# A two-block network on one core: modulation moved into the first mixing, an embedding's projection in fp32 ahead of the FFNs, and the context FFN ended ahead of the second FFN

## The chip, the core and the metric

The kernel runs on one core of a Trainium2 chip. A core has TensorE (matmul, written PE, with its weight load PEld), VectorE (DVE), ScalarE (ACT), GpSimd (POOL) and SyncE (SP, which here issues most of the DMAs). The metric is the device time of one execution in microseconds. Three timed runs of the kernel before gave a median of 2905.65 us (2905.5 to 2906.85).

## The reference

One call takes a latent of 256 tokens of width 1024 through two blocks. `first_block` has two layers:

```python
h = h + mixing(rmsnorm(h))     # layer 0: RWKV recurrence + Hyena; layer 1: neighbourhood attention
h = h + conv_ffn(h, ...)       # (gelu(u[:2816]) * u[2816:]) @ w_down, u = dwconv(rmsnorm(h) @ w_up)
h = h + sigmoid(rmsnorm(h) @ w_gate) * (p_i @ w_proj)      # per-layer embedding, p_i is 256 x 256
```

`second_block` has two layers with a second stream, the context of 256 tokens. Each layer is a half-FFN, a token mixing and another half-FFN, and every norm is modulated:

```python
ml = split(silu(c) @ w_mod[l] + b_mod[l], 9)        # latent; mc is the same with c_ctx, for the context
x   = half_ffn(x,   g_norm[l,0], ml[0], ml[1], ml[2], ...)
ctx = half_ffn(ctx, g_norm[l,0], mc[0], mc[1], mc[2], ...)
```

The modulation needs only `c`, `c_ctx` and `w_mod`, and the context's first half-FFN needs only `ctx` and the modulation. So both can be computed at any time ahead of their use, beside the first block. The same holds for `p_i @ w_proj`.

## The kernel before

**Layout and products.** Activations lie with features on the partitions, as [128, 8, 256] (eight tiles of 128 features by 256 tokens). Nearly every product is made as three matmuls of a reduced-precision fp32 type (`fp32r`). An fp32 weight tile is loaded into a `raw` buffer and split into a high part, a cast on ScalarE (L359), and a low part, a subtraction on VectorE or GpSimd (L360). The activation is split the same way. `gemm` then adds three products: high by high (L368), high by low (L369) and low by high (L370). `gemm_wide` (L406 to L408) does so for four weight tiles at a time, for the start of a stage behind a norm. `plain` (L397) is the other form: the fp32 weight and the fp32 activation go into one matmul as they are, with no split. `plain_tiles` (L372) loads for it and takes its buffers from the pool `self.whole`, 512 columns each.

**Buffers.** From the first FFN on, weights arrive in four `raw` buffers of 128 x 1024 fp32. The split parts lie in pairs `wh`, `wl`: two pairs in `wha`, which live for the whole kernel, and some in `whb`, which a stage opens for itself. PSUM has eight banks; until the first embedding of the second layer is over, four hold the main products (`mm`), two the norms (`aux`) and two the context FFN (`fill`).

**Stages.** `run` (L1437) writes out the first mixing (`mix`), the first FFN (`conv_ffn(0)`), the first embedding (`embed(0)`), the attention (`na`), the second FFN and the second embedding; then come the stages of the second block. A scheduler of the framework orders each engine's instructions by their place in the program and by when their operands and buffers come free in a timeline that it estimates. So work that stands late in the program is drawn forward into gaps. An instruction given to `keep_in_program_order` is not.

**Work drawn forward.** Two kinds of it matter here. The first is the context FFN. `ctx_ffn` (L948) is a generator of eight pieces with its own buffers and PSUM banks. Four pieces (`CUT`) are written last in `mix`; the rest stand behind the second embedding (L1487), so in the program they come after all six first stages, and the scheduler draws them forward. The second is the modulation. `mod_until` (L1004) computes it in steps, 36 a layer. A step loads two tiles of `w_mod` (128 x 1024) and reduces each against `silu(c)` and `silu(c_ctx)`, which lie in `sc` on all partitions. In `mix` the steps 0 to 11 are written ahead of the context FFN, which needs them: each tile comes on GpSimd's DMA queue into a `wha` buffer and takes two reductions on VectorE (L1032). In the FFNs the steps 12 to 19 and 20 to 25 are spread over the groups. There each tile comes on SP's queue into a `wm` buffer. VectorE makes one reduction. The other is a product on GpSimd (L1036), a sum on ScalarE (L1037) and an add on VectorE (L1038). Later stages do the rest of the 72 steps in the same way.

**FFN.** `conv_ffn` (L532) has 22 pairs of up-tiles in three groups. Each pair goes through a convolution over tokens (L527 to L529), gelu, a product and a split (`mh`, `ml`); after a group come its down-products, added to `H` (L568). Ahead of it all stands the norm: `norm1` (L511) takes the root that `rows` makes of the sums of squares (L454), by some small VectorE operations (L424 to L441), spreads it with a matmul against the identity (L480) and scales each tile (L519).

**Embedding.** `embed` (L572) first projects `p_i`: it splits it (`ph`, `pl`), and for each of eight tiles of `ple_p` it loads, splits and multiplies, two chunks deep, then writes half of the product to `pj`. Then comes the norm, the gate's first four tiles in `gemm_wide`, the other four one by one, and the residual add.

Of the kernel before, what the change touches and what calls it, by code (L numbers as in the profile page):

```python
# [10 lines left out]
F32R = mybir.dt.float32r  # L11
I32 = mybir.dt.int32
AF = mybir.ActivationFunctionType
ALU = mybir.AluOpType
# [3 lines left out]
P = 128  # L18
D = 1024
T = 256  # L20
KT = 8
FF = 2816
FT = 22
# [5 lines left out]
DEPTH = 2  # L29
M00 = 32  # L30
CUT = 4
DECAY = math.exp(-0.5)


# [238 lines left out]
class Net:  # L273
# [98 lines left out]
    def plain_tiles(self, name, todo):  # L372


        arr = self.ap[name]
        i = 0
        while i < len(todo):
            t, k0, kn = todo[i]
            n = kn * P
            m = 1  # L380
            while i + m < len(todo) and (m + 1) * n <= 512 and todo[i + m] == (t + m, k0, kn):
                m += 1
            raws = []
            for c in range(0, n, 512):
                w = min(512, n - c)
                raw = self.t(self.whole, [P, 512], "raw")
                src = arr[t : t + m, :, k0 * P + c : k0 * P + c + w].rearrange("t p n -> p t n")
                self.nc.sync.dma_start(raw[:, : m * w].rearrange("p (t n) -> p t n", t=m), src)
                raws.append(raw)
            for j in range(m):  # L390
                yield t + j, lambda k, at=j * n: raws[(at + k * P) // 512][:, (at + k * P) % 512 :][:, :P]
            i += m
# [136 lines left out]
        nc.vector.scalar_tensor_tensor(out[:, 0 : n - 1], src[:, 1:n], w[2], out[:, 0 : n - 1], op0=ALU.mult, op1=ALU.add)  # L529


    def conv_ffn(self, i, mods):  # L532
        nc = self.nc
        with ExitStack() as es:
            pool = self.pool(es, "ffn")
            self.whl_open(es, 0, 3)
            it = self.wtiles(f"f_up{i}", range(2 * FT), KT)
            first = self.first(it, 4)
            xh, xl = self.norm1(pool, f"ffn_norm{i}")
            self.mod_open(pool, True)  # L540
            mod0 = self.mod_at
            outs = [self.acc()[:, :T] for _ in range(4)]
            self.gemm_wide(outs, first, KT, xh, xl)
            for k0, kn in GROUPS:
                mh = self.t(pool, [P, 8, T], "mh", F32R)
                ml = self.t(pool, [P, 8, T], "ml", F32R)
                for j in range(kn):
# [12 lines left out]
                    nc.scalar.activation(u[:, 0], u[:, 0], AF.Gelu_apprx_tanh)  # L560
                    nc.vector.tensor_mul(u[:, 0], u[:, 0], u[:, 1])
                    self.split(u[:, 0], mh[:, j], ml[:, j])
                    if k0 + j > 1:
                        self.mod_until(mod0 + (mods - mod0) * (k0 + j) // (FT - 1))
                for m, wh, wl in self.pieces(f"f_dn{i}", [(m, k0, kn) for m in range(KT)]):
                    ps = self.acc()[:, :T]
                    self.gemm(ps, wh, wl, kn, mh, ml)
# [1 line left out]
                    if k0 == 16:  # L569
                        self.sq_add(m)  # L570

    def embed(self, i):  # L572
        nc = self.nc
        with ExitStack() as es:
            pool = self.pool(es, "ple")
            self.whl_open(es, 0, 3)
            ph = self.t(pool, [P, 2, T], "ph", F32R)
            pl = self.t(pool, [P, 2, T], "pl", F32R)
            pr = self.t(pool, [P, 2, T], "pr")
            nc.sync.dma_start(pr, self.ap[f"p{i}"])  # L580
            self.split(pr, ph, pl)
            pj = self.t(pool, [P, KT, T], "pj")
            m = 0
            for _, wh, wl in self.pieces(f"ple_p{i}", [(t, 0, 2) for t in range(KT)]):
                ps = self.acc()
                self.gemm(ps[:, :T], wh, wl, 2, ph, pl)
                nc.scalar.mul(pj[:, m], ps[:, :T], 0.5)
                m += 1
            it = self.wtiles(f"ple_g{i}", range(KT), KT)
            first = self.first(it, 4)  # L590
            xh, xl = self.norm1(pool, f"ple_norm{i}")
            outs = [self.acc()[:, :T] for _ in range(4)]
            self.gemm_wide(outs, first, KT, xh, xl)
            for m in range(KT):
                if m < 4:
                    ps = outs[m]
                else:
                    ps = self.acc()[:, :T]
                    _, wh, wl = next(it)
                    self.gemm(ps, wh, wl, KT, xh, xl)  # L600
                s = self.t(pool, [P, T], "sg", bufs=2)
                nc.scalar.activation(s, ps, AF.Tanh, scale=0.5)
                nc.vector.scalar_tensor_tensor(s, s, 1.0, pj[:, m], op0=ALU.add, op1=ALU.mult)
                nc.vector.tensor_add(self.H[:, m], self.H[:, m], s)
                self.sq_add(m)

# [232 lines left out]
    def mix(self, ef):  # L839
# [3 lines left out]
        nc = self.nc  # L843
        with ExitStack() as es:
# [4 lines left out]
            with ExitStack() as e2:  # L849
# [82 lines left out]
                self.tag = self.aux = "fill"  # L932
                self.mod_until(12)
                self.rest = self.ctx_ffn(fp)
                for _ in range(CUT):
                    next(self.rest)

    def out0(self, k0, kn, y, last=False):

# [497 lines left out]
    def run(self, es, stages=None):  # L1437
# [30 lines left out]
        self.raw = self.pool(es, "raw", bufs=4)  # L1468
        self.nrm = self.pool(es, "nrm", bufs=6)
        self.rsp = self.pool(es, "rsp", bufs=2)  # L1470
        ep = es.enter_context(ExitStack())
        self.psum_open(ep, mm=4, aux=2, fill=2)
        if "modall" in st:
# [7 lines left out]
                    self.sq_add(k, q)  # L1481
        for s in st:
            if s.startswith("ffn"):
                self.conv_ffn(int(s[3]), 20 if s == "ffn0" else 26)
            elif s.startswith("ple"):
                self.embed(int(s[3]))
                if s == "ple1" and self.own:  # L1487
                    self.tag = self.aux = "fill"
                    for _ in self.rest:
                        pass  # L1490
# [1 line left out]
                    ef.close()  # L1492
                    ep.close()
                    self.psum_open(es, mm=5, aux=3)
            elif s == "na":
                self.na()
            elif s[0] == "h":
# [261 lines left out]
```

## Time and profile before

| | |
|---|---|
| median of three runs | 2905.65 us |
| profiled execution, and its span | 2907.19 us, 2905.4 us |
| granted clock of TensorE | 0.968 |
| busy: PE, DVE, ACT, POOL | 2767.0 us (95%), 1978.3 us (68%), 1216.2 us (42%), 396.7 us (14%) |
| DMA | 143 GB/s in the mean |
| mixing / first FFN / first embedding | to 537 us / 537 to 770 / 770 to 806 |
| attention / second FFN / second embedding | 806 to 1031 / 1031 to 1232 / 1232 to 1262 |
| second block | from 1262 us to the end |

The trace is of one profiled execution. The span goes from the first instruction to the last. An engine's busy time counts the time in which at least one of its instructions ran. The stages' bounds are the times at which TensorE goes over from the one stage's products to the next; work drawn forward from later stages runs inside them.

### The profile page before, as it was taken

To read this page: it belongs to the slowest core of one execution; us is meant where nothing else is said; L and a number is where in the kernel's file an instruction comes from. 1 tells how busy PE (TensorE), PEld (TensorE's weight loads), DVE (VectorE), ACT (ScalarE), POOL (GpSimd) and SP (SyncE) were. 2 spreads that over 40 slices of the span, in tenths; PEclk is the share of its full clock that TensorE was granted. 3 is DMA by queue.
4 is the path that set the end of the run, shared out by engine and by line. 5 is a ranking of instruction groups with operands and counts; after the bars stand their busy time and mean duration, and the time that the engine had idled before them with its cause. 6 is when DMAs were issued, how large, how long until landed. Compare 5 with 4: busy or idle time off the path is not lost.

```text
span 2905.4 us, 49052 instructions
## 1 busy us (share of the span) xinstructions
PE 2767.0 (95%) x19514; PEld 2441.6 (84%) x19514; DVE 1978.3 (68%) x3569; ACT 1216.2 (42%) x2120; POOL 396.7 (14%) x276
## 2 busy tenths in 40 slices
PE   6998999899999989989999999999999999999999
PEld 4676788899899889979988669888898888895999
DVE  5875755789976688867754665777755655567655
ACT  3212223555545555555554454222243222455543
POOL 0100000322542411221211001000010000121100
PEclk8998999999999999989999999999999999999999
DMA  4441223666455356547732103555535444230564
GB/s 164 126 141 58 81 83 117 211 214 221 165 179 159 107 189 203 185 142 241 223 113 68 47 30 119 186 196 179 163 110 164 141 142 134 79 117 25 175 188 139
DMA packets 150807, 415.91 MB, mean 143 GB/s; under 512 B 31585, under 2 KB 51698, under 8 KB 149682
## 3 DMA queue, kind: packets, MB, share of 16 engines
q1 hardware_dynamic: 146258, 393.89, 42.3%
q0 software_dynamic: 4320, 18.88, 1.9%
q8 instruction: 154, 2.52, 0.4%
q14 instruction: 75, 0.61, 0.1%
HBM read 411.66 MB, written 1.05 MB: 142 GB/s over the span
## 4 chain that ended last, share of the span: by engine, by line
PE 73%; DVE 8%; issue 4%; ACT 2%; DMA 1%; POOL 0%; ACTq 0%; DVEq 0%; SPq 0%; POOLq 0%
PE mm L368 18%; PE mm L370 18%; PE mm L369 18%; DVE wl L360 3%; PE fill L370 2%; PE fill L368 2%; PE mm L407 2%; PE mm L1413 2%; PE fill L369 2%; PE mm L408 2%; PE mm L406 2%; PE mm L1381 1%; PE aux L459 1%; ACT wh L359 1%; PE aux L1407 1%
## 5 line engine op out<-in xcount | busy, mean ns | idle before, releaser
L359 ACT CAST wh<-raw 128x1024 fp32r<-128x1024 f32 (+3 forms) x652 | 606.8, 938 | 1016.3 <-PE mm L369 560.8
L360 DVE TENSOR_TENSOR wl<-raw,wh 128x1024 fp32r<-128x1024 f32 (+3 forms) x582 | 712.6, 1228 | 321.3 <-ACT wh L359 308.4
L368 PE MATMUL mm<-xnh,wh 128*128 128x256 f32 (+1 forms) x2592 | 821.4, 317 | 4.2 <-ACT u L527 3.2
L370 PE MATMUL mm<-xnh,wl 128*128 128x256 f32 (+1 forms) x2592 | 818.5, 316 | 1.9 <-DVE wl L360 1.9
L369 PE MATMUL mm<-xnl,wh 128*128 128x256 f32 (+1 forms) x2592 | 815.5, 315 | 0.4 <-DVE xnl L360 0.2
L368 PEld LDWEIGHTS mm<-xnh,wh 128*128 128x128 f32 x2592 | 488.3, 188 | 38.3 <-ACT u L527 3.4
L370 PEld LDWEIGHTS mm<-xnh,wl 128*128 128x128 f32 x2592 | 488.3, 188 | 37.9 <-DVE wl L360 2.9
L369 PEld LDWEIGHTS mm<-xnl,wh 128*128 128x128 f32 x2592 | 487.9, 188 | 34.4 <-DVE xnl L360 1.0
L369 PE MATMUL mm<-ml,wh 128*128 128x256 f32 (+1 forms) x1104 | 341.3, 311 | 10.8 <-DVE ml L360 10.8
L368 PE MATMUL mm<-mh,wh 128*128 128x256 f32 (+1 forms) x1104 | 340.5, 314 | 5.0 <-ACT mh L359 2.1
L370 PE MATMUL mm<-mh,wl 128*128 128x256 f32 (+1 forms) x1104 | 341.0, 312 | 0.0
L1032 DVE CUSTOM_DVE_ANT_0 junk<-wm,sc,vecs 128x1024 bf16<-128x1024 f32 x200 | 256.8, 1284 | 4.2 <-ACT sc L1015 1.1
L369 PEld LDWEIGHTS mm<-ml,wh 128*128 128x128 f32 x1104 | 208.4, 189 | 25.2 <-DVE ml L360 12.2
L368 PEld LDWEIGHTS mm<-mh,wh 128*128 128x128 f32 x1104 | 206.3, 189 | 18.5 <-ACT mh L359 2.9
L370 PEld LDWEIGHTS mm<-mh,wl 128*128 128x128 f32 x1104 | 208.2, 189 | 13.3
L360 POOL TENSOR_TENSOR wl<-raw,wh 128x1024 fp32r<-128x1024 f32 (+2 forms) x70 | 134.2, 1925 | 370.6 <-DMA raw<-s_up 190.9
L496 POOL TENSOR_TENSOR ss<-ss,xt 128x256 f32<-128x256 f32 x56 | 58.9, 1058 | 889.1 <-issue 689.3
L1036 POOL TENSOR_TENSOR wm<-wm,sc 128x1024 f32<-128x1024 f32 x40 | 109.9, 2747 | 432.3 <-DVE mod L1032 346.6
L1107 DVE SCALAR_TENSOR_TENSOR H<-mm,mod,H 128x256 f32<-128x256 f32 x112 | 53.7, 482 | 116.7 <-PE mm L370 116.6
L1154 DVE TENSOR_TENSOR sg<-sg,mm 128x256 f32<-128x256 f32 (+1 forms) x88 | 48.7, 553 | 123.1 <-PE mm L370 120.8
L407 PE MATMUL mm<-xnl,wh 128*128 128x256 f32 x416 | 121.3, 299 | 7.9 <-DVE xnl L1058 4.9
L408 PE MATMUL mm<-xnh,wl 128*128 128x256 f32 x416 | 120.1, 295 | 3.9 <-DVE wl L360 2.0
(549 smaller groups left out, 4386.9 us busy)
## 6 DMA issues: line engine op xcount, KB each, us to landing
raw<-s_up SPq DMA_DIRECT2D x220, 512.0 KB, 3.7
wm<-w_mod SPq DMA_DIRECT2D x120, 512.0 KB, 4.4
raw<-f_up SPq DMA_DIRECT2D x88, 512.0 KB, 4.5
raw<-s_dn SPq DMA_DIRECT2D x65, 512.0 KB, 3.5
raw<-s_dn SPq DMA_DIRECT2D x60, 384.0 KB, 3.1
raw<-w_in SPq DMA_DIRECT2D x34, 512.0 KB, 3.6
raw<-f_dn SPq DMA_DIRECT2D x32, 512.0 KB, 4.4
raw<-w_in SPq DMA_DIRECT2D x52, 256.0 KB, 3.0
```

What stands on the lines that cost most here:

```text
L359: self.nc.scalar.copy(hi, src)
L360: (self.nc.gpsimd if pool or self.own and self.tag == "fill" else self.nc.vector).tensor_sub(lo, src, hi.bitcast(F32))
L368: nc.tensor.matmul(out, wh[:, ws], h, start=first and k == 0, stop=False)
L369: nc.tensor.matmul(out, wh[:, ws], l, start=False, stop=False)
L370: nc.tensor.matmul(out, wl[:, ws], h, start=False, stop=last and k == kt - 1)
L406: nc.tensor.matmul(out, wh[:, s], h, start=k == 0, stop=False)
L407: nc.tensor.matmul(out, wh[:, s], l, start=False, stop=False)
L408: nc.tensor.matmul(out, wl[:, s], h, start=False, stop=k == kt - 1)
L496: (nc.gpsimd if self.tag == "mm" else nc.vector).tensor_add(self.ss[s], self.ss[s], x)
L1032: keep(nc.vector.tensor_tensor_reduce(out=junk, in0=w, in1=self.sc[:, i], scale=0.5 if self.half else 1.0, scalar=self.vecs[:, b + t : b + ...
L1036: nc.gpsimd.tensor_mul(w, w, self.sc[:, 1])
L1413: nc.tensor.matmul(po[64 * h : 64 * h + 64, :T], v(k0 // P + i), pTs[h][:, i], start=i == 0, stop=i == nk // P - 1)
```

## The change

The diff has three parts.

1. `MODS` is 26. In `mix` each of the four context pieces is now followed by some modulation steps: up to step 15, 19, 22 and 26. They use the form that `mix` had for the steps 0 to 11, with GpSimd's queue, the `wha` buffers and four reductions on VectorE. The calls of `mod_open` and `mod_until` in `conv_ffn` are gone.
2. The projection of `p_i` moves from `embed` to a new function, `project_embedding`, which `conv_ffn` calls ahead of its own weights. It takes the weights as fp32 (`plain`), loads two tiles in one DMA, uses the `raw` pool (whose buffers in `plain_tiles` become as large as the others of that pool), and keeps `pj` in a pool `pj` that lives until the second embedding is over.
3. The rest of the context FFN is written ahead of the second FFN and not behind the second embedding, and PSUM is laid out anew there: five banks for `mm` and three for `aux`.

```diff
+MODS = 26
@@ plain_tiles
-                raw = self.t(self.whole, [P, 512], "raw")
+                raw = self.t(self.whole, [P, 512 if self.tag == "in" else 1024], "raw")
@@
-    def conv_ffn(self, i, mods):
+    def conv_ffn(self, i):
             self.whl_open(es, 0, 3)
+            self.project_embedding(i)
             it = self.wtiles(f"f_up{i}", range(2 * FT), KT)
             first = self.first(it, 4)
             xh, xl = self.norm1(pool, f"ffn_norm{i}")
-            self.mod_open(pool, True)
-            mod0 = self.mod_at
...
-                    if k0 + j > 1:
-                        self.mod_until(mod0 + (mods - mod0) * (k0 + j) // (FT - 1))
+    def project_embedding(self, i):
+        nc = self.nc
+        pr = self.t(self.pjp, [P, 2, T], "pr")
+        nc.sync.dma_start(pr, self.ap[f"p{i}"])
+        self.pj = self.t(self.pjp, [P, KT, T], "pj")
+        for m, w in self.plain_tiles(f"ple_p{i}", [(t, 0, 2) for t in range(KT)]):
+            ps = self.acc()
+            self.plain(ps[:, :T], w, 2, pr)
+            nc.scalar.mul(self.pj[:, m], ps[:, :T], 0.5)
@@ embed
-            ph = self.t(pool, [P, 2, T], "ph", F32R)
-            pl = self.t(pool, [P, 2, T], "pl", F32R)
-            pr = self.t(pool, [P, 2, T], "pr")
-            nc.sync.dma_start(pr, self.ap[f"p{i}"])
-            self.split(pr, ph, pl)
-            pj = self.t(pool, [P, KT, T], "pj")
-            m = 0
-            for _, wh, wl in self.pieces(f"ple_p{i}", [(t, 0, 2) for t in range(KT)]):
-                ps = self.acc()
-                self.gemm(ps[:, :T], wh, wl, 2, ph, pl)
-                nc.scalar.mul(pj[:, m], ps[:, :T], 0.5)
-                m += 1
@@ mix
-                for _ in range(CUT):
+                for i in range(CUT):
                     next(self.rest)
+                    self.mod_until(12 + (MODS - 12) * (i + 1) // CUT)
@@ run
+        self.whole = self.raw
+        fb = es.enter_context(ExitStack())
+        self.pjp = self.pool(fb, "pj")
@@
-                self.conv_ffn(int(s[3]), 20 if s == "ffn0" else 26)
-            elif s.startswith("ple"):
-                self.embed(int(s[3]))
-                if s == "ple1" and self.own:
+                if s == "ffn1" and self.own:
                     self.tag = self.aux = "fill"
                     for _ in self.rest:
                         pass
...
                     self.psum_open(es, mm=5, aux=3)
+                self.conv_ffn(int(s[3]))
+            elif s.startswith("ple"):
+                self.embed(int(s[3]))
+                if s == "ple1":
+                    fb.close()
```

## Rows read from the trace of the kernel before

**Rows 1.** Cores: span and mean granted TensorE clock.

```profile
core 0: 2905.4 us, clock 0.968
```

**Rows 2.** Stretches: length, busy us (instructions) of PE, PEld, DVE, ACT, POOL; PEclk, DMA share, GB/s.

```profile
102.00:190.00 88.00, 79.89 (x900) 61.95 (x900) 87.52 (x169) 13.62 (x29) 10.63 (x20) 0.98 0.58 183
190.00:240.00 50.00, 49.73 (x477) 40.02 (x475) 17.22 (x45) 7.21 (x15) 0.00 (x0) 0.90 0.23 71
240.00:300.00 60.00, 49.49 (x279) 36.34 (x278) 36.01 (x97) 18.34 (x37) 0.00 (x0) 0.75 0.12 38
...
340.00:495.00 155.00, 153.00 (x1774) 137.35 (x1775) 89.33 (x189) 44.00 (x80) 0.53 (x1) 0.96 0.31 97
537.00:770.00 233.00, 217.84 (x1793) 215.57 (x1792) 211.05 (x312) 137.29 (x225) 83.15 (x38) 0.98 0.64 214
770.00:806.00 36.00, 31.91 (x226) 30.75 (x225) 24.45 (x42) 17.97 (x37) 14.28 (x7) 0.86 0.46 162
1031.00:1232.00 201.00, 189.73 (x1573) 187.31 (x1572) 171.44 (x262) 116.90 (x187) 34.77 (x16) 0.99 0.58 192
1232.00:1262.00 30.00, 23.58 (x159) 22.80 (x159) 19.54 (x40) 15.47 (x34) 6.61 (x3) 0.83 0.39 127
```

**Rows 3.** Stretches: 100 us of the second block's first FFN.

```profile
1300.00:1400.00 100.00, 100.00 (x852) 100.00 (x851) 74.11 (x93) 57.72 (x82) 19.97 (x6) 1.00 0.71 236
```

**Rows 4.** Tiles sc and w_mod, 102 to 190 us: reductions min/median/max ns; landing of loads.

```profile
L1032 DVE CUSTOM_DVE_ANT_0 junk<-wl,sc,vecs x24: 1262/1276/1286, 107.5 to 188.6; 128x1024 bf16<-128x1024 f32 x24
...
DMA to landing us min/median/max: 3.6/3.9/5.7
```

**Rows 5.** Tile wm, all stages: GpSimd's products, ns min/median/max, first and last start.

```profile
L1036 POOL TENSOR_TENSOR wm<-wm,sc x40: 2380/2422/3429, 592.2 to 1471.7; 128x1024 f32<-128x1024 f32 x40
```

**Rows 6.** Timeline of POOL, then DVE, in the first FFN: start us, us, operation.

```profile
649.29 2.41 POOL L1036 TENSOR_TENSOR wm<-wm,sc 128x1024 f32<-128x1024 f32 x1 [24.70 <-DVE mod L1032]
...
649.13 0.08 DVE L1032 DVE_READ_ACCUMULATOR2_ANT mod<- 128x1 f32 x1
...
649.52 3.26 DVE L360 TENSOR_TENSOR wl<-raw,wh 128x1024 fp32r<-128x1024 f32 x1
...
653.61 1.22 DVE L360 TENSOR_TENSOR wl<-raw,wh 128x1024 fp32r<-128x1024 f32 x1
```

**Rows 7.** Waits of PE, first FFN, then second: total us, times, longest.

```profile
PE mm L369 <- DVE ml L360: 6.1, 4, 2.9
...
PE mm L369 <- DVE ml L360: 4.7, 3, 3.5
PE mm L368 <- ACT u L527: 3.2, 1, 3.2
```

**Rows 8.** Tile raw and timeline of PE in the mixing: fp32 products with x.

```profile
L397 PE MATMUL in<-x,raw x64: 379/379/484, 304.2 to 323.9; 128*128 128x256 f32 x64
...
309.58 3.72 PE L397 MATMUL in<-x,raw 128*128 128x256 f32 x16
```

**Rows 9.** Timeline at the start of the second embedding.

```profile
1230.92 2.25 DVE L360 TENSOR_TENSOR wl<-raw,wh 128x256 fp32r<-128x256 f32 x1
...
1235.35 0.61 PE L454 MATMUL aux<-c_sums,xt 128*128 128x2 f32 x4 [2.85 <-ACT xt L491]
...
1240.72 0.38 PE L480 MATMUL aux<-c_ident,rsyaux 128*128 128x128 f32 x2
```

**Rows 10.** Timeline at the start of the first FFN.

```profile
536.93 0.59 PE L454 MATMUL aux<-c_sums,xtin 128*128 128x2 f32 x4
...
537.54 1.75 SPq L322 DMA_DIRECT2D raw<-f_up  x4
...
541.89 0.69 PE L480 MATMUL aux<-c_ident,rsyaux 128*128 128x128 f32 x2 [4.04 <-DVE rsyaux L441]
```

**Rows 11.** Tile f_up ahead of the second FFN: loads issued, first and last.

```profile
L322 SPq DMA_DIRECT2D raw<-f_up x9: 328/328/373, 1001.7 to 1022.2; - x9
```

**Rows 12.** Tile fill: down-products of the context FFN, first and last.

```profile
L368 PE MATMUL fill<-mh,wh x176: 277/283/553, 401.7 to 1028.4; 128*128 128x256 f32 x176
```

More of the change, by code (lines that the diff above doesn't have):

```diff
@@ L602, in embed @@
                 nc.scalar.activation(s, ps, AF.Tanh, scale=0.5)
-                nc.vector.scalar_tensor_tensor(s, s, 1.0, pj[:, m], op0=ALU.add, op1=ALU.mult)
+                nc.vector.scalar_tensor_tensor(s, s, 1.0, self.pj[:, m], op0=ALU.add, op1=ALU.mult)
                 nc.vector.tensor_add(self.H[:, m], self.H[:, m], s)
```

## The prediction

> **What bounds the kernel now.** I read the span and the clock first: one core, 2905.4 us, granted clock 0.968 [rows 1]. The profiled execution took 2907.19 us, so 1.8 us lie outside the span; the three timed runs have a median of 2905.65 us, 1.5 us less. The sums below are differences, and I take them from the median.
>
> Then the table of busy time by stretch, cut at the stages that the change touches [rows 2]. The reader should see two things. TensorE is busy nearly everywhere, but its busy time counts matmuls that overlap, so I count matmuls instead. In a stretch of the second half without any wait, 852 matmuls of 256 columns run in 100 us, which is 117.4 ns each [rows 3]. By that measure the first FFN (537 to 770) needs 1793 x 0.1174 = 210.5 us and takes 233, so 22.5 us are lost; the second FFN (1031 to 1232) needs 184.7 of 201, 16.3 lost; the two embeddings (770 to 806, 1232 to 1262) need 26.5 of 36 and 18.7 of 30, 9.5 and 11.3 lost. The other thing is VectorE: it is busy for 211 of 233 us in the first FFN (91%) and 171 of 201 in the second (85%). In the stretch without a wait it is at 74% [rows 3]. TensorE is the bound, and where it loses time in the FFNs it mostly waits for VectorE: 6.1 and 4.7 us on the subtraction that ends a split of an activation, and 3.2 us for a PSUM bank [rows 7].
>
> **Modulation out of the FFNs.** Steps 12 to 25 leave: 8 from the first FFN, 6 from the second. A step has there two products on POOL of 2.42 us and two reductions on VectorE of 1.28 us [rows 4, 5], with two reads of 0.08 [rows 6] and two small adds, by my estimate 0.15 each since they are as small: 3.0 us of VectorE. That frees 24 us of it in the first FFN and 18 in the second. There is a second relief: while POOL works at a product (649.29 to 651.70) a VectorE subtraction takes 3.26 us, which takes 1.22 right after [rows 6]. So each of the 28 products can hold VectorE for up to 2.04 us; it need not meet one. With about 1.3 us each, VectorE in the first FFN falls from 211 to about 211 - 24 - 21 = 166 us, near 74% of what the stage would then take, the share at which TensorE ran without a gap [rows 3]. ScalarE and the loads are lightened too, but nobody waits for those. The gain lies between nothing (the waits are the ends of chains, not load) and all that is lost, 22.5 + 16.3 = 38.8. I take a little under half, 10 and 8 us: at a group's end the last conv, gelu and split still have to come one after another. The 8 hold the PSUM wait of 3.2, since from the second FFN on the main product has five banks instead of four.
>
> **The same steps in the mixing.** There a step has no POOL product: four reductions, 4 x (1.28 + 0.08) = 5.4 us, 14 steps 76 us of VectorE. Where do they go? Steps 0 to 11 stand last in the program's order too, and they ran from 102 to 189 [rows 4], filling VectorE to 87.5 of 88 us [rows 2]: 7.3 us a step. The new ones will follow: 14 x 7.3 = 103 us, to about 293. In that time VectorE now stands idle for 33 us (190 to 240) and about 21 (of 240 to 293) [rows 2], 54 together. So 54 us of the 76 hide in VectorE's gaps, and TensorE, which sets the pace from 190 to 240 (49.7 of 50), does not feel them. 22 us do not fit. They push back operations of the recurrence and of the Hyena part, of which TensorE waits for some; about half lies on that path, and I take 10 us. Bounds: nothing, if the steps spread on to 340 and beyond, where 66 us of 155 are free; 22, if all that does not fit is paid. Below nothing is excluded: the mixing gets work and loses none. What is late next: the weights of the context FFN, which use the same two buffer pairs from about 305 on. If the last steps still hold one of them then, the first pieces load singly; I count that within the 22.
>
> **The projection.** The old one: 8 tiles x 2 x 3 = 48 matmuls of 117.4 ns [rows 3], 5.6 us a block, behind 8 casts, 8 subtractions and a split of the input. The new one takes fp32 weights as they are. The old trace has such products in the mixing: its 32 with x stand as 64 records, two a product, and 16 records take 3.72 us [rows 8], so a product takes 465 ns, 16 of them 7.4 us. On TensorE the projection gets dearer by 1.8 us a block; what counts is what it lies beside.
> At the embedding it goes away, 2 x 5.6 = 11.3 us of TensorE, and with it the splits that stand ahead of the gate's weights and of the norm: in the second block one of these subtractions takes 2.25 us with the last residual add behind it, and from the last sum (1235.35) to the spread of the root (1240.72) go 5.4 us [rows 9]. The gate's first four tiles no longer wait for buffers that the projection holds. From the 9.5 and 11.3 us lost there I take 3 us each. Bounds: nothing, if the projection only filled the wait for the norm; 11.3 + 20.8 = 32, if all of it goes. I take 17, nearer to the row with the matmuls, since these are surely gone while the norm's own chain stays.
> At the FFN it is added, 2 x 7.4 = 14.9 us. At the first FFN TensorE waits 4.0 us for the root [rows 10], and the start of the second has the same wait, shorter. But the queue matters: SP issues four loads of the projection and one of its input ahead of the FFN's first weights, and these four take all four raw buffers. The first FFN's loads go out at 537.54 [rows 10] and can't go earlier, as the buffers lie where the mixing's last squares are read; now the first will go out some 6 us later, when the projection gives buffers back, and behind them wait four casts on ScalarE and four subtractions on VectorE and POOL, for which the wide product waits. In the second FFN the loads went out from 1001.7 [rows 11], 20 us early, so some slack is there. The context FFN's pieces cover part of this in the first. Bounds: nothing (all beside waits) to 14.9 + 2 x 6 = 27. I take 7: half of the matmuls, the late loads beside the norm.
>
> **The context FFN.** Its matmuls ended at 1028 already [rows 12], before the second FFN's product got going. It stands last behind the mixing, the first FFN, the first embedding and the attention both before and after; only a tail of a few pieces moves ahead. I cost it at nothing (up to 4 us if the attention has more of it to carry).
>
> **Sum.** +10 (mixing) + 7 (projection added) - 17 (projection gone) - 18 (FFNs) = -18 us: 2887.6, say 2888.
>
> **Rivals.**
> A: the FFNs' waits are not VectorE's load but the chain at a group's end, and the second FFN gets only the bank. Then -18 becomes -5, the rest as above: -5, about 2903 to 2901. For it: the wait on the split of an activation comes in four and three pieces with one of 2.9 and one of 3.5 us, at the group's ends [rows 7]. Against: 91% of VectorE.
> B: the mixing hides all of the steps and the FFNs reach the rate of rows 3 nearly: 0 + 7 - 17 - 25 = -35, 2871. For it: 33 + 24 + 66 us of free VectorE in the stretches from 190 to 300 and from 340 to 495 [rows 2]. Against: the stretch 240 to 300 has a clock of 0.75, a sign of a chain that waits already.
> C, slower: the steps get no buffers. They take them from the pairs that the context FFN's weights use, and a step that has not got its pair by 305 must share: while it holds one (a landing of 3.9 us and two reductions, some 7 us), that FFN has one pair, and each of its tiles shows a cast and a subtraction of 2.3 us. The steps of the last group stand behind all context pieces of the mixing, and the first FFN's buffers lie over the scale vector that they read, so it can't begin before they end. Price: 10 steps x 7 us, of which a third shows, 23, and four at the end, 4 x 5.4 = 22: +45 in place of +10, the sum +17, 2923. It decides from a longer mixing of 28 us on. For it: with that FFN's products TensorE is busy for 153 of 155 us from 340 to 495 [rows 2], so any hole there is paid. Against: steps 0 to 11 were drawn forward by more than 200 us.
> On the loads of C the Trainium skill has a rule ("SBUF — State Buffer", section "SBUF: two separate sides"): loads issued from GpSimd's queue starve while VectorE runs certain operations, since descriptors can't be written. It gives 620 ns that become 3100, an estimate of 2.5 us more for each of the 28 new loads. This trace does not show it: the twenty loads issued under a VectorE at 99% landed in 3.6 to 5.7 us, median 3.9 [rows 4]. By that rule C would be likelier; by the row it stays at its chance.
>
> **How the numbers follow.** The forecast as summed, 2877 to 2899: 0.46. A 0.20, B 0.17, C 0.17. The prediction is that of the first, 2888. For 8 in 10 the range takes in B and A with the bounds of the mixing and leaves out most of C: 2868 to 2913. Within 0.2% (5.8 us) is what a measurement of this kernel can't tell from no change, 2899.8 to 2911.5. Faster: the first, B, and a third of A, 0.70. Same: the rest of A, 0.13. Slower: C, 0.17.
>
> **What would show it.** Reductions of the steps without a break from 102 to about 290 or 340, and none after 537 until the second half; the time at which the first FFN's sums stand (now 536.9 [rows 10]) later by 0 to 22 us. In the FFNs no product on POOL, subtractions of 1.2 us, the wait for the split of an activation under 2 us. The first FFN's first load later behind the projection, 16 fp32 products beside the wait for the root. At the embeddings from the last sum to the gate's first matmul under 8 us. Wrong, if reductions run between 495 and 537, if the gap ahead of the first FFN grows beyond 10 us, or if the FFNs' waits stay.

## The result, and the profile after

The changed kernel took 2937.45 us (median of 4 runs, 2933.99 to 2940.44), the kernel before 2905.98 us beside it: a ratio of 1.0108, interval 1.009 to 1.0125. It is 31.5 us slower. The prediction was 2888, faster, and its range of 2868 to 2913 does not hold the time.

Span and clock of the profiled execution (2940.44 us), against [rows 1]:

```profile
core 0: 2938.7 us, clock 0.962
```

The table of stretches comes next, cut where the stages now lie: end of the mixing with the context pieces (420 to 625), first FFN (625 to 840), first embedding, second FFN (1080 to 1264), second embedding.

```profile
190.00:240.00 50.00, 49.75 (x503) 40.14 (x502) 18.49 (x47) 7.21 (x15) 0.00 (x0) 0.93 0.24 75
240.00:300.00 60.00, 49.78 (x282) 36.52 (x281) 36.74 (x98) 18.35 (x37) 0.00 (x0) 0.77 0.12 38
...
420.00:495.00 75.00, 59.64 (x432) 51.98 (x430) 50.63 (x111) 17.95 (x36) 5.85 (x11) 0.88 0.51 166
495.00:540.00 45.00, 30.15 (x215) 28.68 (x216) 34.44 (x56) 12.25 (x20) 2.00 (x4) 0.79 0.46 141
540.00:580.00 40.00, 23.03 (x164) 22.00 (x163) 28.31 (x46) 9.79 (x15) 2.78 (x6) 0.79 0.51 167
580.00:625.00 45.00, 31.38 (x219) 29.31 (x218) 41.30 (x58) 11.34 (x18) 24.59 (x17) 0.89 0.59 202
625.00:840.00 215.00, 211.54 (x1766) 210.18 (x1767) 161.39 (x255) 124.62 (x198) 34.46 (x21) 1.00 0.63 200
840.00:866.00 26.00, 23.55 (x195) 22.97 (x195) 18.46 (x37) 11.64 (x23) 10.80 (x7) 1.00 0.36 112
...
1080.00:1264.00 184.00, 179.59 (x1497) 178.89 (x1497) 137.12 (x225) 101.11 (x159) 2.35 (x1) 0.97 0.56 176
1264.00:1290.00 26.00, 17.93 (x126) 16.76 (x125) 17.49 (x39) 12.80 (x23) 9.54 (x6) 0.79 0.49 162
```

Three things are to be seen against [rows 2]. From 190 to 300 VectorE stands as idle as before: the new steps are not there. From 420 to 625 TensorE makes only 1030 matmuls in 205 us, and its granted clock is 0.79 to 0.89; before, this work was over at 537. And the FFNs did become shorter: at 117.4 ns a matmul [rows 3] the first loses 215 - 207 = 8 us and the second 184 - 176 = 8, where before they lost 22.5 and 16.3. By the stages' bounds here and in the kernel before, the mixing is 88 us longer, the two FFNs are 18 and 17 us shorter, the embeddings 10 and 4, the attention 11, and the second block is 5 us longer: 33 us of span.

Where the steps went stands in the view of their loads between 415 and 640 us (first and last issue, what GpSimd had waited for, the landing), in GpSimd's timeline at the first load of three of the four blocks, and in the view of the reductions (52 on `wl`, 24 of them of the steps 0 to 11):

```profile
L1027 POOL DMA_DIRECT2D wh<-w_mod x14: 530/530/579, 423.1 to 605.9; - x14
...
  PE fill L371: 374.9, 6
...
DMA to landing us min/median/max: 3.7/4.6/7.5
```

```profile
486.19 0.53 POOL L1027 DMA_DIRECT2D wh<-w_mod  x1 [49.94 <-PE fill L371]
...
539.59 0.53 POOL L1027 DMA_DIRECT2D wh<-w_mod  x1 [37.18 <-PE fill L371]
...
587.55 0.53 POOL L1027 DMA_DIRECT2D wh<-w_mod  x1 [37.26 <-PE fill L371]
```

```profile
L1030 DVE CUSTOM_DVE_ANT_0 junk<-wl,sc,vecs x52: 1266/1285/3260, 108.4 to 625.0; 128x1024 bf16<-128x1024 f32 x52
```

All 28 loads were issued between 423 and 611 us, in four blocks, and each block began when the context FFN's last matmul with the pair was over (`PE fill`). The last reduction began at 625.0. What TensorE and ScalarE waited for from 420 to 650 (total us, times, longest):

```profile
PE fill L369 <- ACT wh L360: 31.3, 5, 17.0
PE fill L371 <- DVE wl L361: 7.7, 3, 3.2
PE aux L481 <- DVE rsyaux L442: 6.3, 1, 6.3
PE fill L371 <- POOL wl L361: 5.4, 4, 1.8
```

```profile
ACT wh L360 <- DVE mod L1030: 45.2, 6, 14.7
```

The chain is plain: the cast of the context FFN's next weights waits for the reduction that still reads the pair (45.2 us in six pieces), and TensorE waits for the cast (31.3 us).

Behind it, a wait of the DMA queue at the projection's loads, the first FFN's loads, against [rows 10], and the largest waits of TensorE in the two FFNs, against [rows 7]: none on the split of an activation is left among them.

```profile
SPq L389 <- DVE mod L1030: 6.9, 1, 6.9
```

```profile
L323 SPq DMA_DIRECT2D raw<-f_up x88: 327/328/412, 628.6 to 1234.6; - x88
```

```profile
PE mm L398 <- DMA raw<-ple_p: 1.5, 1, 1.5
PE mm L369 <- DVE u L530: 1.4, 1, 1.4
...
PE aux L481 <- DVE rsyaux L442: 5.1, 1, 5.1
PE mm L407 <- ACT xnh L360: 4.0, 1, 4.0
```

### The profile page after: what moved, and what is told of

It is laid out like the page before. It is cut to its first block, busy times and chain, and to the rows that moved or that the text cites. A ratio compares the mean times of both kernels' runs of the same rounds, so it can differ in the third digit from the quotient of the medians.

```text
span 2938.7 us, 48867 instructions
## 1 busy us (share of the span) xinstructions
PE 2763.4 (94%) x19482; PEld 2437.4 (83%) x19482; DVE 1963.6 (67%) x3575; ACT 1180.7 (40%) x2042; POOL 330.6 (11%) x274
## 4 chain that ended last, share of the span: by engine, by line
PE 71%; DVE 7%; issue 3%; ACT 1%; DMA 1%; SPq 0%; DVEq 0%; ACTq 0%; POOLq 0%
PE mm L371 19%; PE mm L369 19%; PE mm L370 19%; PE mm L408 2%; PE mm L1411 2%; PE mm L409 2%; PE mm L407 2%; PE mm L1379 1%; DVE wl L361 1%; PE aux L460 1%; DVE junk L1030 1%; PE fill L371 1%; PE fill L369 1%; PE fill L370 1%; PE aux L1405 1%
## 5 line engine op out<-in xcount | busy, mean ns | idle before, releaser
L361 DVE TENSOR_TENSOR wl<-raw,wh 128x1024 fp32r<-128x1024 f32 (+3 forms) x566 | 664.8, 1177 | 357.5 <-ACT wh L360 346.1
L1030 DVE CUSTOM_DVE_ANT_0 junk<-wm,sc,vecs 128x1024 bf16<-128x1024 f32 x172 | 220.3, 1281 | 3.7 <-ACT sc L1013 1.3
L369 PE MATMUL fill<-xnh,wh 128*128 128x256 f32 x352 | 106.6, 303 | 30.6 <-ACT wh L360 30.4
L371 PE MATMUL fill<-xnh,wl 128*128 128x256 f32 x352 | 108.5, 309 | 14.3 <-DVE wl L361 7.7
```

Source lines behind the costliest of these rows:

```text
L361: (self.nc.gpsimd if pool or self.own and self.tag == "fill" else self.nc.vector).tensor_sub(lo, src, hi.bitcast(F32))
L369: nc.tensor.matmul(out, wh[:, ws], h, start=first and k == 0, stop=False)
L371: nc.tensor.matmul(out, wl[:, ws], h, start=False, stop=last and k == kt - 1)
L1030: keep(nc.vector.tensor_tensor_reduce(out=junk, in0=w, in1=self.sc[:, i], scale=0.5 if self.half else 1.0, scalar=self.vecs[:, b + t : b + ...
```

## The experiments

Each kernel is the changed one or the one before with the edit shown. Ratios are to the kernel before, run beside it. The first four ask where the 31 us come from.

**e1, the steps written first.** In `mix` of the changed kernel:

```diff
-                self.mod_until(12)
+                self.mod_until(MODS)
                 self.rest = self.ctx_ffn(fp)
-                for i in range(CUT):
+                for _ in range(CUT):
                     next(self.rest)
-                    self.mod_until(12 + (MODS - 12) * (i + 1) // CUT)
```

> The changed kernel with the steps 12 to 25 written ahead of the context FFN, right behind step 11, and none behind its pieces. Theory B (buffers): in the changed kernel these steps ran in four blocks from 424 to 625 us, each behind a piece of the context FFN, because they take the same two wh/wl pairs as its weights, in the order of the program; TensorE stood still in the mixing for some 60 us more than before. Written first they should run from 190 to about 295 us in VectorE's gaps, the first FFN's loads go out at about 540 to 550 instead of 628, and the time is 2937 - 55 = 2882 (2870 to 2895). Rival L (load): 76 us of VectorE work lengthen the mixing wherever they stand; then the first FFN's loads go out after 600 and the time stays over 2920.

Measured: 2897.25 us, 0.9977 (0.9966 to 0.9988). Of the time 40 us are gone by the order alone, so rival L falls. Yet it is 2 us over the range given: the steps ran in the gaps, but not for nothing. Reductions, the first FFN's first load, the two stretches in which the load on VectorE shows, and the second of them in the kernel before:

```profile
L1029 DVE CUSTOM_DVE_ANT_0 junk<-wl,sc,vecs x52: 1264/1276/1286, 106.6 to 323.5; 128x1024 bf16<-128x1024 f32 x52
```

```profile
L323 SPq DMA_DIRECT2D raw<-f_up x88: 327/328/425, 555.4 to 1192.6; - x88
```

```profile
240.00:300.00 60.00, 45.18 (x224) 30.24 (x225) 51.85 (x118) 15.68 (x31) 5.90 (x11) 0.69 0.42 135
300.00:340.00 40.00, 38.36 (x254) 29.94 (x254) 31.37 (x69) 7.22 (x13) 0.53 (x1) 0.78 0.30 96
```

```profile
300.00:340.00 40.00, 38.08 (x394) 29.78 (x392) 29.56 (x66) 11.02 (x20) 0.00 (x0) 0.99 0.28 88
```

Against the changed kernel VectorE goes from 37 to 52 us in the 60 from 240 on. TensorE makes 224 matmuls there and not 282, and its granted clock is 0.69 and not 0.77; from 300 to 340 it is 0.78, and 0.99 in the kernel before.

**e2, buffers of their own.** Changed kernel, order kept:

```diff
+            mown = self.pool(es, "mown", bufs=3)
...
                 self.mod_until(12)
+                self.modw = mown
...
-                    w = self.t(self.modw, [P, D], ("wh", "wl")[j])
+                    w = self.t(self.modw, [P, D], "wh" if self.mod_at > 12 else ("wh", "wl")[j])
```

> The changed kernel, its order in the program kept, but the steps 12 to 25 load into three buffers of their own (128 x 1024) instead of the wh/wl pairs. Theory B (buffers): nothing of the context FFN stands between a step and its buffer any more, so the steps are drawn forward to between 190 and 340 us and the time is that of the steps written first, 2882 (2870 to 2898). Rival O (order): the steps stay behind their pieces because they are written there, whatever buffers they have; they run after 400 still. With O the pairs are at least not held by them, and the time is 2905 to 2930. Rival L (load): over 2920.

Measured: 2914.05 us, 1.0042 (1.0026 to 1.0058). Reductions and one wait of TensorE from 280 to 345:

```profile
L1032 DVE CUSTOM_DVE_ANT_0 junk<-wh,sc,vecs x80: 1262/1270/1285, 103.4 to 318.3; 128x1024 bf16<-128x1024 f32 x80
```

```profile
PE b L1607 <- DVE e L1605: 11.5, 1, 11.5
```

The steps stand in the same place of the program as in the changed kernel, and ran up to 300 us earlier, done by 320. That is theory B's mechanism, and rival O falls by the place, though the time lies in the range that O gave: it was the pair that held the steps back, not their place in the program. The time is 16 us over B's range. A part of that is seen: TensorE waited 11.5 us for the recurrence's small VectorE operation on L1605, and in that time VectorE did three reductions (3.8 us) among other operations. In the profiled executions e2 is 8 us behind e1 at the first FFN's sums (556.3 against 548.7) and 14 at the second's (1046.5 against 1032.2). Why it is so is not shown.

**e3, the steps alone.** The kernel before with the first part of the change: in `mix` each `next(self.rest)` is followed by `self.mod_until(12 + (MODS - 12) * (i + 1) // CUT)`; in `conv_ffn` the calls of `mod_open` and `mod_until` are taken out.

> The kernel before with the first part of the change alone: the steps 12 to 25 behind the context pieces in the mixing and none in the FFNs; projection and context FFN stay where they were. Theory B: the whole loss comes with this part, +60 in the mixing and -20 to -25 in the FFNs, so 2940 (2930 to 2952). Rival P (the projection, or the new place of the context FFN, costs what was lost): below 2915.

Measured: 2943.45 us, 1.015 (1.0128 to 1.0171). Inside theory B's range: the whole loss lies in this part, and rival P falls.

**e4, the steps left out.** The changed kernel with no step behind the pieces.

```diff
                 self.mod_until(12)
+                nc.vector.memset(self.mod[:, 0, 24:52], 0.5)
+                self.mod_at = 26
...
-                    self.mod_until(12 + (MODS - 12) * (i + 1) // CUT)
```

> The changed kernel with the steps 12 to 25 left out altogether: the modulation of these columns is set to a constant, so that part of the computation is missing. It gives the price of the steps in the changed kernel. Theory B: 2937 less 55 to 65, about 2877 (2868 to 2888), and at most 15 us below the run with the steps written first. Rival L: the same time here, but over 35 us below the run with the steps written first. If it stays over 2915, the loss comes from other parts of the change.

Measured: 2882.25 us, 0.9933 (0.9916 to 0.995). That is inside theory B's range. So the 14 steps cost 55 us where the change puts them (2937.45 - 2882.25; 51 by the two ratios) and 15 us where e1 has them (13 by the ratios).

The traces of e1 and e4 show that the 15 us have two sources. The attention's last product ends at 999.2 in e1 and at 989.7 in e4: 9.5 us come from the mixing, where the load on VectorE is seen. From there to the second FFN's last sum pass 33.0 us in e1 and 22.4 in e4: in e1 the context FFN had fallen behind beside the slower mixing, and 155 of its matmuls, not 82, were left for this place.

**e5 and e6, the other parts alone.** The kernel before with `project_embedding` and its call (e5), or with the rest of the context FFN and `psum_open(es, mm=5, aux=3)` ahead of `conv_ffn(1)` (e6).

> The kernel before with the second part of the change alone: the projection as fp32 products ahead of the FFNs, all else as before. My prediction had +7 at the FFNs and -17 at the embeddings, -10, so 2896. The run with the steps alone (2943) against the whole change (2937) leaves some -6 for the two other parts together. Theory G (gain): 2892 to 2902. Rival Z (zero): the loads behind the projection's raw buffers and the dearer products eat what the embeddings win, within 4 us of the kernel before, 2901 to 2909.

> The kernel before with the third part of the change alone: the rest of the context FFN written ahead of the second FFN, which then has five PSUM banks. My prediction had nothing for the place, and 3.2 us for the PSUM wait within the second FFN's 8: 2902 (2899 to 2906). Rival: a tail of context pieces that used to run inside the second FFN's or embedding's gaps now stands alone, 2907 or more.

Measured: e5 2906.29 us, 0.9992 (0.9983 to 1.0001); e6 2906.44 us, 0.9998 (0.9985 to 1.001). Neither can be told from no change. For the projection my -10 was wrong and rival Z right; e6 lies between its range and its rival's, and as it also moves the PSUM layout, the two aren't separated.

**e7, the kernel before without the steps.** The calls of `mod_open` and `mod_until` in `conv_ffn` are taken out, and in `mix`:

```diff
                 self.mod_until(12)
+                nc.vector.memset(self.mod[:, 0, 24:52], 0.5)
+                self.mod_at = 26
```

> The kernel before with the steps 12 to 25 left out (their columns are set to a constant, so that part of the computation is missing): what the FFNs gain by being rid of them, with nothing paid in the mixing. My prediction had -18 for this; the gaps between matmuls in the two FFNs of the changed kernel were 15 and 9 us shorter than before. By the prediction 2888; by the gaps 2882 (2876 to 2886); by its rival A (the waits are the chains at a group's end) 2900.

Measured: 2874.93 us beside 2908.78, 0.9875 (0.9856 to 0.9894): 34 us. The FFNs' stretches and their largest waits but the norm's:

```profile
537.00:745.00 208.00, 202.64 (x1695) 202.03 (x1695) 161.08 (x251) 114.85 (x181) 30.51 (x15) 0.98 0.61 190
...
1008.00:1202.00 194.00, 192.53 (x1649) 192.36 (x1648) 146.36 (x238) 107.00 (x176) 14.95 (x14) 1.00 0.57 172
```

```profile
PE mm L408 <- POOL wl L360: 1.4, 2, 1.0
...
PE mm L368 <- DVE u L529: 1.5, 1, 1.5
```

VectorE falls from 91% and 85% to 77% and 75%, the second FFN runs at 117.6 ns a matmul, and the wait on the split is gone. Rival A falls, and my -18 was about half of it.

**e8, e1 with the old projection.**

> The run with the steps written first (2897), with the projection put back into the embeddings as it was. If the projection's part brings 10 us (Theory G), 2907; if it is worth nothing (Rival Z), 2897 (2893 to 2901).

Measured: 2899.09 us, 0.997 (0.9959 to 0.9982), against 0.9977 for e1: rival Z again.

**e9 and e10, half a step each.** The kernel before, its 14 FFN steps cut to the loads and GpSimd's products (e9) or to the loads and VectorE's reductions (e10).

> The kernel before, where each of the 14 FFN steps keeps its two loads and its two GpSimd products, but has no reduction on VectorE and no sum on ScalarE (the columns are set to a constant, so that part of the computation is missing). Without the steps at all the kernel took 34 us less than before. Theory K (the products hold VectorE up): over half of the 34 comes back, 2893 to 2906. Theory V (VectorE's own 3 us a step are what was lost): under 10 us come back, 2872 to 2884.

> The kernel before, where each of the 14 FFN steps keeps its two loads and its two VectorE reductions against one vector, but has no GpSimd product, ScalarE sum or add (the other columns are set to a constant, so that part of the computation is missing). Theory V: over half of the 34 us comes back, 2893 to 2906. Theory K: under 10 us come back, 2872 to 2884. With neither over half, the two load VectorE together.

Measured: e9 2880.38 us, 0.9905 (0.9885 to 0.9926); e10 2880.94 us, 0.9908 (0.9879 to 0.9936). Neither theory alone: each part brings back about 9 us of the 34 (0.9905 and 0.9908 against 0.9875), and with intervals of 0.002 to 0.003 on each ratio, 9 us is hardly clear of nothing. The other 16 us may come from the two together, or from the sum on ScalarE and the small add on VectorE, which neither run has; no run separates these.

**e11 and e12, the step count.** e1 with `MODS = 20`, so that the steps 20 to 25 fall to the second block's first FFN (e11); or with those six in three buffers of their own behind the first three pieces, kept in program order (e12).

> The run with the steps written first, but only steps 12 to 19 there; the steps 20 to 25 go to the second block's first FFN, which spreads 12 steps over its groups and not 6. VectorE stood idle for 33 us from 190 to 240, where TensorE lost nothing, and 8 steps are 43 us. Theory L (in the mixing the steps cost by VectorE's load, from about 240 us on): the mixing is only 5 us longer than without steps, the second block's FFN, at 74% of VectorE, takes 6 steps of 3 us for 0 to 8 us, in sum 2888 (2880 to 2894). Rival: steps cost the same wherever they stand (1 to 2.4 us each), 2895 or more.

> As the run before, but the steps 20 to 25 stay in the mixing: two behind each of the first three context pieces, in three buffers of their own and kept in VectorE's program order, so that they run between 340 and 540 us, where VectorE had 66 us free in 155. Theory B and L: no pair is held and VectorE has room, so 0 to 8 us for the six, 2886 (2878 to 2894). Rival: a reduction kept in order stands on VectorE until its load has landed (some 6 us), and the context FFN's subtractions wait behind it: six steps x 6 us, 2905 or more.

Measured: e11 2882.96 us, 0.9924 (0.9909 to 0.9939), inside its range; e12 2899.25 us, 0.9977 (0.9965 to 0.9988), over its own and under its rival's. e11 is as fast as the kernel that leaves the 14 steps out (e4). A part of that is not the steps' doing: in its profiled execution the last FFN, which none of these steps touches, is 8 us shorter than in e4 (190 us from its last sum to the end, against 198). At a granted clock of 1.00 in both, 179 matmuls stand in 20 us of it and not 172 (2760 to 2780); why is open. The other 9 us of e12's 16 come from ahead of it. The second FFN's last sum stands at 1031.8 in e12 and at 1018.2 in e11, and from the attention's last product to it 125 context matmuls ran and not 82: the context FFN had fallen behind here too. No pair was held, but from 480 to 540 VectorE is busy for 55 of 60 us, and for 39 in e11.

**e13 and e14, what the light FFNs uncover.** e4 leaves out the same steps as e7 and was still 17 us slower against its kernel before. e7 with the projection's part (e13), or with the context FFN's (e14):

> The kernel before without the steps 12 to 25 (their columns constant, so that part of the computation is missing) and with the projection in fp32 ahead of the FFNs; the context FFN as before. Without the steps, neither of the two other parts gave a ratio of 0.9875 to the kernel before, both gave 0.9933: 17 us dearer, where each alone, with the steps in the FFNs, gave -2.5 and -0.6. Theory I (it is the projection: with VectorE relieved its fp32 products and late loads are no longer hidden by other waits): 0.992 to 0.994, about 2885. Rival J (it is the context FFN's place): 0.986 to 0.989, about 2872.

> The kernel before without the steps 12 to 25 (their columns constant, so that part of the computation is missing) and with the context FFN ended ahead of the second FFN; the projection as before. In the run without steps 87 of the context FFN's matmuls (10 us) ran behind the second FFN's first products; here they must run ahead of it. Theory J: they then stand alone at the attention's end, 0.991 to 0.994, about 2883. Rival I: 0.986 to 0.989, about 2872. If both runs lie between, the two share it.

Measured: e13 2876.79 us, 0.9904 (0.9889 to 0.992); e14 2888.95 us, 0.9946 (0.9931 to 0.9961). e13 lies between the ranges of its two theories and e14 a little over J's. Most of it is the third part, rival J, though a little may be the projection's: 0.9904 to 0.9875 is at the edge of the two intervals. e14 moves the context FFN and lays out PSUM anew, which no run separates. In the view of the context FFN's down-products the last one of e7 runs at 1208.6, behind the second FFN's last product; that of e14 at 1015.9:

```profile
L368 PE MATMUL fill<-mh,wh x176: 274/283/775, 401.5 to 1208.6; 128*128 128x256 f32 x176
```

```profile
L368 PE MATMUL fill<-mh,wh x176: 277/283/775, 401.0 to 1015.9; 128*128 128x256 f32 x176
```

In e14 the attention's last product ends at 989.4, and then 155 context matmuls run to the end before the norm's sums, whose bank belongs to the new layout, begin (1016.28); from the one to the last sum pass 27 us, and 4.5 in e7. Behind them stands the norm with nothing beside it, where e7 still had 42 context matmuls. e14's timeline of TensorE:

```profile
1016.64 1.48 PE L454 MATMUL aux<-c_sums,xt 128*128 128x2 f32 x12
1023.04 0.69 PE L480 MATMUL aux<-c_ident,rsyaux 128*128 128x128 f32 x2 [4.92 <-DVE rsyaux L441]
1024.74 1.22 PE L406 MATMUL mm<-xnh,wh 128*128 128x256 f32 x4 [1.01 <-ACT xnh L359]
...
1027.19 0.42 PE L407 MATMUL mm<-xnl,wh 128*128 128x256 f32 x1
1027.40 0.41 PE L408 MATMUL mm<-xnh,wl 128*128 128x256 f32 x1
```

From the last sum to the first product pass 8 us, as in e7, but 4.9 of them TensorE waits for the root. The matmuls that follow stand 0.21 us apart, against 0.12 later, the lower of the clock's two levels (1.2 and 2.4 GHz); the granted clock from 1020 to 1040 is 0.76 there.

**e15 and e16, eight first without the other parts.** The kernel before with `mod_until(20)` ahead of the context FFN and no step in `conv_ffn`; e16 has the projection's part besides.

> The kernel before with the steps 12 to 19 written ahead of the context FFN in the mixing and the steps 20 to 25 left to the second block's first FFN, as in the run with eight first, but without the two other parts of the change. That run gave 0.9924 with both. If the two parts cost some 17 us once the FFNs are rid of the steps, 0.987 to 0.989, about 2870; if they cost nothing, 0.9915 to 0.994.

> The run before with the projection in fp32 ahead of the FFNs, the context FFN as before. Theory I: 5 us or more above it, 0.990 to 0.993. Rival J: within 4 us of it or below.

Measured: e15 2875.49 us, 0.9895 (0.9879 to 0.9911); e16 2881.26 us, 0.9917 (0.9898 to 0.9936). The first lies just above the range that the cost of the two parts gave, and clearly below the other. The second is 6 us above it by the medians, which by its expectation is theory I, the projection; but the intervals overlap. e13 and e16 give the projection a cost of 8 and 6 us, e5 and e8 none: it stays open. e15 does all of the work and is the fastest such kernel here: 29 us less than the kernel before, 62 less than the changed one. Its stretches: the eight steps in the gap, and the six in the second block's first FFN.

```profile
190.00:240.00 50.00, 47.71 (x496) 38.92 (x491) 45.20 (x96) 6.70 (x14) 6.89 (x13) 0.96 0.65 212
240.00:300.00 60.00, 54.16 (x304) 39.64 (x303) 45.00 (x113) 18.64 (x38) 0.00 (x0) 0.70 0.11 36
...
1251.00:1448.00 197.00, 192.60 (x1608) 191.61 (x1608) 175.67 (x223) 116.83 (x185) 82.26 (x32) 0.99 0.66 226
```

VectorE is filled from 17 to 45 us of the first 50, and TensorE makes 496 matmuls in it as against 477. The first FFN's sums stand at 535.6, in e7, which has no steps, at 538.0.

## Why the prediction was wrong, by its own steps

The sum by the runs, each ratio taken against the one before it: the FFNs rid of the steps -1.25% (e7); the context FFN's place on top of that +0.71% (e14); the projection on top of both -0.13% (e4, within the intervals); the steps behind the pieces +1.75% (the whole change). That makes +1.08%.

**The same steps in the mixing** is the step that failed. "The new ones will follow: 14 x 7.3 = 103 us, to about 293": the first was loaded from 423 on, and the last reduction began at 625. I took the steps 0 to 11 as the pattern, "last in the program's order too". But those stand ahead of the context FFN in the program, and the new ones behind its pieces; the pairs go from user to user in that order, so an instruction can be drawn forward only as far as its buffer lets it. With other buffers (e2) or another place (e1) the same 14 steps did go to where I had them. +10 was forecast, with 22 as the far bound; the runs have 55 us. Even where the steps do go into the gaps they cost 15, so +10 was a fair size for a thing that did not happen. About 10 of the 15 are VectorE's load from 240 us on; the eight steps that fit ahead of it can't be told from free (e15's sums against e7's). The rest is the context FFN set back, which the sum did not have.

**Rival C** named the place, the pairs and the point that the first FFN can't get its buffers before the last step: the projection's loads, the first of that stage, waited 6.9 us for a reduction (SPq L389 above), and the FFN's own first load went out at 628.6, behind the last reduction at 625.0. Its price, 45 in place of 10, is near the 55. Its chance, 0.17, rested on the wrong "against". It still gave 2923, because other terms were off too, as follows.

**Modulation out of the FFNs**: the direction was right, the size half of what was there, -34 for -18. The step that failed is "at a group's end the last conv, gelu and split still have to come one after another": they do, but with VectorE at 77% no wait on the split is left. The bound of all that is lost, 38.8, was the nearer end. GpSimd's products and VectorE's reductions are each worth about 9 us alone (e9, e10); where the other 16 come from stays open.

**The context FFN** "at nothing" was right for the kernel before (e6) and wrong for the changed one (e14, 21 us). Without the steps in the FFNs 155 of its matmuls were left at the attention's end, and ending them there held up the second FFN's sums by 19 us and left its root uncovered. In e7 they run beside that norm and behind it, and the second FFN is 7 us longer for it (197 us from its first product to its last, 190 in e14). I looked at where the tail ran before, not at where it would run after another part of the same change.

**The projection**: -10 forecast, nothing measurable alone (e5). Both of its terms were mis-sized. e5's last sums and first products at the two FFNs:

```profile
539.82 0.59 PE L454 MATMUL aux<-c_sums,xtin 128*128 128x2 f32 x4
...
556.20 0.28 PE L406 MATMUL mm<-xnh,wh 128*128 128x256 f32 x1
...
1018.03 0.50 PE L454 MATMUL aux<-c_sums,xt 128*128 128x2 f32 x4
...
1031.32 1.05 PE L406 MATMUL mm<-xnh,wh 128*128 128x256 f32 x4
```

From the one to the other pass 16.4 and 13.3 us; in the kernel before 9.9 (536.93 to 546.78) and 7.2 (1019.56 to 1026.73). So the +7 measured about 13. At the embeddings the same way falls from 15.7 and 8.4 us to 12.4 and 6.8, and from the last down-product to the gate's last one from 52.6 and 41.8 to 43.4 and 39.9: the -17 measured some 11, with different amounts of context work beside it. The time under 8 us that I named as a sign came at the second embedding of the changed kernel (6.5 us, 1279.26 to 1285.75) and not at the first, with context matmuls beside it:

```profile
838.43 0.50 PE L455 MATMUL aux<-c_sums,xt 128*128 128x2 f32 x4
...
849.36 0.63 PE L407 MATMUL mm<-xnh,wh 128*128 128x256 f32 x4
```

These are single executions, and e5 and the kernel before differ by less than such executions scatter, so the sizes are rough.

**The rule on loads from GpSimd's queue**: the 28 new loads landed in 3.7 to 7.5 us, median 4.6, 0.7 over the median of [rows 4]. By the rule of the Trainium skill ("SBUF — State Buffer", section "SBUF: two separate sides") the estimate was 2.5 us more for each. No run here shows that.

## What to carry to other kernels

Work that a scheduler draws forward goes no further than its buffer lets it: before a step is costed into an idle engine's gap, look up who holds its buffer, in the program's order, right before it. An idle share is spent from the start: eight steps fitted into the stretch in which VectorE stood idle and TensorE lost nothing, and the next six cost 1 to 3 us each (e1 and e12 against e11, with and without its short last FFN). Work that runs in the background has to end somewhere: what slows it in one stage is paid where its rest stands alone. And where one part of a change removes waits, cost the other parts in the kernel without them: what used to run in those waits has to go somewhere.

## What was not expected of the hardware

A reduction on VectorE is held by GpSimd as a subtraction is [rows 6]. In the changed kernel GpSimd's subtraction begins at 601.78 and takes 2.61 us; of VectorE's reductions the one that begins inside it takes 3.29 us, its neighbours 1.28.

```profile
601.78 2.61 POOL L361 TENSOR_TENSOR wl<-raw,wh 128x1024 fp32r<-128x1024 f32 x1
```

```profile
600.86 1.28 DVE L1030 CUSTOM_DVE_ANT_0 junk<-wh,sc,vecs 128x1024 bf16<-128x1024 f32 x1
...
602.18 3.29 DVE L1030 CUSTOM_DVE_ANT_0 junk<-wh,sc,vecs 128x1024 bf16<-128x1024 f32 x1
...
605.51 1.28 DVE L1030 CUSTOM_DVE_ANT_0 junk<-wl,sc,vecs 128x1024 bf16<-128x1024 f32 x1
```

The Trainium skill ("SBUF — State Buffer", section "SBUF: two separate sides") has it that a VectorE operation with two SBUF inputs and a GpSimd operation that reads SBUF take a shared pair of ports in turn, whole instructions at a time. The trace agrees: 3.29 is 1.28 and most of the 2.21 us that GpSimd's operation still had to run (602.18 to 604.39).
